# Seven block products in a feed-forward layer: when a chunk's weights are split, where one of their sums lies, and which engine adds one sum

## The chip, the cores and the metric

The kernel runs on one core of a Trainium2 chip. Its engines work side by side, each through its own instructions in order: TensorE (PE, with its weight loads as PEld), VectorE (DVE), ScalarE (ACT), GpSimd (POOL) and SyncE (SP), which issues most DMAs. The metric is the time of one execution in microseconds (us) of the device; lower is better.

## The reference, cut to what matters

The program computes two blocks one after the other; the change lies in the last layer of the second, in its feed-forward part:

```python
def swiglu(h, w_gate, w_up, w_down):
    return (jax.nn.silu(h @ w_gate) * (h @ w_up)) @ w_down

h_lat = h_lat + m_lat[5] * swiglu(modulate(rms_norm(h_lat), m_lat[3], m_lat[4]),
                                  w_ffn_gate[i], w_ffn_up[i], w_ffn_down[i])
```

There are 512 tokens, the width is 1024 and the inner width 2816. Everything is float32.

## The kernel before, in words

**Split products.** A float32 product is made of three matmuls. Each operand is split into a high part (an ACT cast, L239) and a low part (a DVE subtraction, L240), and PE adds high by high, low by high and high by low. `K.split` makes the two parts, `K.wcut` makes them in two tiles (`wh`, `wl`) of a ring for weights, `K.wraw` loads raw weights into a tile (`wr`) of the same kind of ring, and `K.w4` takes such a tile for other data. All three rings are short: an instruction that needs a tile waits until the last reader of the one it replaces is done, and a load is issued only then.

**Chunks.** The inner width is cut into 11 chunks of 256. `gate_up(c)` makes the 256 inner rows of a chunk, in two halves of 128 (`m` = 2c, called A here, and 2c + 1, called B), and leaves them split in `hidh`, `hidl`. `down(c)` multiplies them by the chunk's down weights: eight PSUM results `ob` (four groups of 128 tokens by two halves of the output), each of six matmuls of 512 columns, and each added to `acc` by DVE (L1632). `run` calls `gate_up(c + 1)` before `down(c)`. `ob` has two PSUM buffers, so the third `ob` needs the first to be added to `acc`.

**Seven products.** In this layer (`seven=True`) the weights of an `m` (gate `g`, up `u`, each 1024 by 128) and the tokens (two halves of 256) form a product of 2 by 2 blocks, and it is done with seven block products in place of eight, each of 12 matmuls of 256 columns. `sums` makes the sums of token blocks once (`t1` to `t4`). `prep(m)` makes the sums of weight blocks on POOL: `sb` (L1510), two halves of `sa` (L1511, L1512) and a new low half of `u` (L1513), and splits them. `seven_up(m)` issues the products (PSUM tiles `wa11`, `wa12`, `ws2`, `ws3`, `ws1`, `ws4`, `wa22`) and adds them into c11, c12 (tile `sg`) and c21, c22 (tile `su`): copies on ACT (L1538, L1542 into `m5`), additions from PSUM on DVE (L1539, L1540, L1541, L1546, L1547), and two additions of `m5` on POOL (L1544, L1545). Then come silu on ACT (L1548), the product with c21, c22 on DVE (L1549) and the split into `hidh`, `hidl`.

**What sets the order.** A scheduler arranges each engine's instructions from the order in which the code writes them and from readiness; the result is fixed before the run. `prep(m + 1)` is written in the middle of `seven_up(m)`. The first chunk is done by plain products (`cb`); the chunk before the last ends with POOL's work on `acc` and the residual (L1634, L1635), and the last chunk's down weights are multiplied by the gate on POOL (L955).

Of the kernel before, what the change touches and what calls it, by code (L numbers as in the profile page):

```python
# [7 lines left out]
F32 = mybir.dt.float32  # L8
F32R = mybir.dt.float32r
# [3 lines left out]
ALU = mybir.AluOpType  # L13
# [4 lines left out]
P = 128  # L18
# [8 lines left out]
DFF = 2816  # L27
# [131 lines left out]
class K:  # L159
    def __init__(self, tc, I, out, ctx):  # L160
        self.tc, self.nc, self.I, self.out = tc, tc.nc, I, out
        self.const = ctx.enter_context(tc.tile_pool(name="const", bufs=1))
        self.wp = ctx.enter_context(tc.tile_pool(name="wp", bufs=1))
        self.dram = ctx.enter_context(tc.tile_pool(name="dramp", bufs=1, space=DRAM))
        self.NR, self.NH = 6, 4
        self.nwork = 0
        self.mixed = True
        self.share = False
        self.nl = 0
        self.nrms = 0  # L170
        self.ident = self.load_const("ident")

        self.res = self.const.tile([P, NT, D], F32, name="res")
        self.mhalf = self.const.tile([P, 16], F32, name="mhalf")
        self.nc.gpsimd.memset(self.mhalf, -0.5)
# [134 lines left out]
    def block1(self, mix):  # L310
# [28 lines left out]
        def add(n):  # L339
            for _ in range(n):  # L340
                next(sums, None)
# [1091 lines left out]
GD = (0,)  # L1433


class FFN:


# [11 lines left out]
    def norm(self, si, hs, hn, pool, npool, tag, bufs, ps=None):  # L1450
        nt, row = self.seqs[si]
        w = nt * P
        h, l = ([pool.tile([P, 4 * w], F32R, name=f"{n}{si}{j}", tag=f"fa{si}", bufs=4) for j in range(2)] for n in ("fh", "fl"))
        vh, vl = (lambda k, a=a: a[k // 4][:, (k % 4) * w:(k % 4) * w + w] for a in (h, l))
        self.xs[si] = vh, vl, w
        keep = None
        if self.seven:

            self.F = [[pool.tile([P, 4, 256], F32, name=f"xf{i}{j}", tag="xf", bufs=5) for j in range(2)] for i in range(2)]
            keep = lambda k, pair: self.F[k // 4][pair][:, k % 4, :]  # L1460
        yield from self.K.norm_T(hs, hn, nt, self.layer, 1, row, vh, vl, npool, ps or self.ps, tag, bufs, keep)

    def open(self, pool):
        self.pool = self.hpool = pool
        n = self.off[-1]
        self.acc = [pool.tile([P, D], F32, name=f"acc{tt}", tag="acc", bufs=n) for tt in range(n)]
# [18 lines left out]
    def sums(self):  # L1485

        V, G = self.nc.vector, self.nc.gpsimd
        (f11, f12), (f21, f22) = self.F
        G.tensor_tensor(f11, f12, f11, ALU.subtract)
        V.tensor_tensor(f12, f22, f12, ALU.subtract)  # L1490
        G.tensor_tensor(f22, f22, f11, ALU.subtract)
        V.tensor_tensor(f21, f21, f22, ALU.subtract)
        vh, vl, w = self.xs[0]
        blk = lambda i, j: lambda k: tuple(v(4 * i + k)[:, j * 256:j * 256 + 256] for v in (vh, vl))
        self.B = dict(b11=blk(0, 0), b21=blk(1, 0), b22=blk(1, 1))
        for n, t in (("t3", f12), ("t2", f22), ("t4", f21), ("t1", f11)):
            h = self.hpool.tile([P, 4, 256], F32R, name="xh" + n, tag="xh", bufs=4)
            l = self.pool.tile([P, 4, 256], F32R, name="xl" + n, tag="xf", bufs=5)
            self.K.split(t, h, l)
            self.B[n] = lambda k, h=h, l=l: (h[:, k, :], l[:, k, :])  # L1500

    def prep(self, m):

        if m in self.preps or m >= DFF // P:
            return
        K, G = self.K, self.nc.gpsimd
        g, u = (K.wraw(self.I[n][self.layer, m], (8, P)) for n in ("w_fg", "w_fu"))
        sa, sb = K.w4("sa").rearrange("p (k c) -> p k c", c=P), K.w4("sb")[:, :512].rearrange("p (k c) -> p k c", c=P)
        lo, hi = slice(0, 4), slice(4, 8)
        G.tensor_tensor(sb, u[:, lo], u[:, hi], ALU.add)  # L1510
        G.tensor_tensor(sa[:, lo], sb, g[:, lo], ALU.subtract)  # L1511
        G.tensor_tensor(sa[:, hi], g[:, lo], u[:, lo], ALU.subtract)  # L1512
        G.tensor_tensor(u[:, lo], g[:, hi], sa[:, lo], ALU.subtract)  # L1513
        gs = K.wcut(g, (8, P))
        sh, sl = (self.hpool.tile([P, 8, P], F32R, name=n, tag=n, bufs=2) for n in ("sah", "sal"))
        K.split(sa, sh, sl)
        ss = K.wcut(sb, (4, P))
        us = K.wcut(u, (8, P))
        part = lambda t, o: lambda k: (t[0][:, o + k, :], t[1][:, o + k, :])
        self.preps[m] = dict(a11=part(gs, 0), a12=part(gs, 4), s3=part((sh, sl), 4), s2=part((sh, sl), 0),  # L1520
                             s4=part(us, 0), a22=part(us, 4), s1=part(ss, 0))

    def seven_up(self, m, hid, mi):

        K, ps, pool = self.K, self.ps, self.pool
        V, S, G = self.nc.vector, self.nc.scalar, self.nc.gpsimd
        self.prep(m)
        A, B, w = self.preps.pop(m), self.B, 256

        def product(a, t):  # L1530
            b = ps.tile([P, 512], F32, name="w" + a, tag="gu", bufs=6)[:, :w]
            for k in range(4):
                K.mm3(b, A[a](k), B[t](k), k == 0, k == 3)
            return b
        t, v = (pool.tile([P, 512], F32, name=n, tag="ntf", bufs=3) for n in ("sg", "su"))
        m5 = self.hpool.tile([P, w], F32, name="m5", tag="kp", bufs=1)
        (c11, c12), (c21, c22) = ((a[:, :w], a[:, w:]) for a in (t, v))
        S.copy(c12, product("a11", "b11"))  # L1538
        V.tensor_tensor(c11, c12, product("a12", "b21"), ALU.add)  # L1539
        V.tensor_tensor(c12, c12, product("s2", "t2"), ALU.add)  # L1540
        V.tensor_tensor(c21, c12, product("s3", "t3"), ALU.add)  # L1541
        S.copy(m5, product("s1", "t1"))  # L1542
        self.prep(m + 1)
        G.tensor_tensor(c12, c12, m5, ALU.add)  # L1544
        G.tensor_tensor(c22, c21, m5, ALU.add)  # L1545
        V.tensor_tensor(c12, c12, product("s4", "b22"), ALU.add)  # L1546
        V.tensor_tensor(c21, c21, product("a22", "t4"), ALU.add)  # L1547
        S.activation(t, t, AF.Silu)  # L1548
        V.tensor_tensor(t, t, v, ALU.mult)  # L1549
        K.split(t, hid[0][:, mi, :], hid[1][:, mi, :])  # L1550

    def gate_up(self, c):
        K, I, nc, ps, pool = self.K, self.I, self.nc, self.ps, self.pool
        hid = tuple(self.hpool.tile([P, 2, self.off[-1] * P], F32R, name=n, tag=n, bufs=2) for n in ("hidh", "hidl"))
        if self.seven and c:
            for mi in range(2):
                self.seven_up(2 * c + mi, hid, mi)
            return hid
        jobs = []
        for mi in range(2):  # L1560
            pre = self.pre[mi] if c == 0 and self.pre else None
            W = pre[0] if pre else self.weights(2 * c + mi)
            for si in reversed(range(len(self.xs))):
                if si and pre:
                    o, w = self.off[si] * P, self.xs[si][2]
                    K.split(pre[1], hid[0][:, mi, o:o + w], hid[1][:, mi, o:o + w])
                else:
                    jobs.append((mi, si, W))
        if c == 0 and not self.pre:
            jobs = [(*j, h) for h in (slice(0, 256), slice(256, 512)) for j in jobs]  # L1570
        for mi, si, W, *cut in jobs:
            vh, vl, w = self.xs[si]
            t0 = cut[0].start if cut else 0
            w = 256 if cut else w
            sl = slice(t0, t0 + w)
            o = self.off[si] * P + t0
            if w == 512:
                out = [ps.tile([P, 512], F32, name="gb", tag="gu", bufs=6) for _ in range(2)]
            else:
                cb = ps.tile([P, 2, 256], F32, name="cb", tag="gu", bufs=6)  # L1580
                out = [cb[:, 0], cb[:, 1]]
            for Wt, b in zip(W, out):
                for k in range(8):
                    K.mm3(b, (Wt[0][:, k, :], Wt[1][:, k, :]), (vh(k)[:, sl], vl(k)[:, sl]), k == 0, k == 7)
            t = pool.tile([P, 512], F32, name="sg", tag="ntf", bufs=3)[:, :w]
            nc.scalar.activation(t, out[0], AF.Silu)
            nc.vector.tensor_tensor(t, t, out[1], ALU.mult)
            K.split(t, hid[0][:, mi, o:o + w], hid[1][:, mi, o:o + w])
        return hid
# [662 lines left out]
```

## Time and profile before

| | us |
|---|---|
| median of 3 runs (lowest, highest) | 2409.57 (2403.1, 2412.35) |
| the profiled execution | 2407.82 |
| its span (first to last instruction) | 2406.0 |
| the part of the span with this layer's chunks, and the normalisation ahead of them | 1957 to 2406 |
| eight equal chunks in it | 2050.45 to 2350.35 |

The span is that of one profiled execution; what lies between it and the execution's time is not in the trace. Rows with a time at their start give start and duration of an instruction, and in brackets how long its engine had been idle and which work of which engine ended that. A granted clock of 1.00 is TensorE's level of 2.4 GHz, 0.50 is 1.2 GHz.

### The profile page before, as it was taken

To read this page: it belongs to the slowest core of one execution; us is meant where nothing else is said; L and a number is where in the kernel's file an instruction comes from. 1 tells how busy PE (TensorE), PEld (TensorE's weight loads), DVE (VectorE), ACT (ScalarE), POOL (GpSimd) and SP (SyncE) were. 2 spreads that over 40 slices of the span, in tenths; PEclk is the share of its full clock that TensorE was granted. 3 is DMA by queue.
4 is the path that set the end of the run, shared out by engine and by line. 5 is a ranking of instruction groups with operands and counts; after the bars stand their busy time and mean duration, and the time that the engine had idled before them with its cause. 6 is when DMAs were issued, how large, how long until landed. Compare 5 with 4: busy or idle time off the path is not lost. (4 is left out here: it accounts for less than half of the span.)

```text
span 2406.0 us, 32156 instructions
## 1 busy us (share of the span) xinstructions
PE 2263.3 (94%) x12468; PEld 1730.6 (72%) x12468; DVE 1535.2 (64%) x2511; ACT 840.7 (35%) x1466; POOL 603.4 (25%) x453
## 2 busy tenths in 40 slices
PE   9999899998889978899999999989999988998987
PEld 7667755433567846788888888868767578888886
DVE  7867642524655787675777544665677757667666
ACT  4344422231433242522112111254456534333332
POOL 0011310242330175300000002520211154434346
PEclk9999999999899987999999999999999999988988
DMA  8655698998832012342444311222000232223221
GB/s 290 233 186 181 236 355 333 393 387 308 309 138 70 20 53 97 105 158 88 149 156 151 114 62 53 79 74 88 1 1 1 78 141 71 88 71 101 78 94 44
DMA packets 99160, 339.02 MB, mean 141 GB/s; under 512 B 14373, under 2 KB 16293, under 8 KB 99002
## 3 DMA queue, kind: packets, MB, share of 16 engines
q1 hardware_dynamic: 94394, 324.33, 37.9%
q0 software_dynamic: 4608, 12.59, 1.5%
q8 instruction: 99, 1.62, 0.3%
q14 instruction: 59, 0.48, 0.1%
HBM read 323.21 MB, written 17.86 MB: 142 GB/s over the span
## 5 line engine op out<-in xcount | busy, mean ns | idle before, releaser
L239 ACT CAST wh<-wr 128x1024 fp32r<-128x1024 f32 (+1 forms) x239 | 248.1, 1046 | 515.7 <-PE ob L243 227.7
L240 DVE TENSOR_TENSOR wl<-wr,wh 128x1024 fp32r<-128x1024 f32 (+1 forms) x235 | 316.4, 1353 | 152.2 <-ACT wh L239 149.5
L243 PE MATMUL ob<-wh,hidh 128*128 128x512 f32 x440 | 177.6, 407 | 24.6 <-ACT wh L239 21.6
L243 PE MATMUL ob<-wl,hidh 128*128 128x512 f32 x440 | 176.8, 405 | 8.0 <-DVE wl L240 7.9
L243 PE MATMUL ob<-wh,hidl 128*128 128x512 f32 x440 | 175.2, 401 | 0.0
L1632 DVE TENSOR_TENSOR acc<-acc,ob 128x512 f32<-128x512 f32 x160 | 108.3, 685 | 95.8 <-PE ob L243 95.8
L877 DVE SCALAR_TENSOR_TENSOR adacc<-wr,cond,adacc 128x512 f32<-128x512 f32 x224 | 152.7, 745 | 1.7 <-DMA wr<-in_w_ada 1.7
L1634 POOL TENSOR_TENSOR acc<-acc,gate 128x1024 f32<-128x1024 f32 x10 | 28.1, 2814 | 472.5 <-DVE acc L1632 472.5
L243 PE MATMUL gb<-fh,wh 128*128 128x512 f32 x352 | 139.3, 396 | 0.0
L243 PE MATMUL gb<-fh,wl 128*128 128x512 f32 x352 | 139.2, 396 | 0.0
L243 PE MATMUL gb<-fl,wh 128*128 128x512 f32 x352 | 139.2, 395 | 0.0
L290 POOL TENSOR_TENSOR rs_r<-rs_v,mhalf 128x1 f32<-128x1 f32 (+1 forms) x54 | 47.4, 882 | 328.0 <-DVE rs_v L288 327.8
L243 PE MATMUL gu<-mw,xgT 128*64 128x512 f32 x512 | 125.3, 603 | 0.9 <-issue 0.7
L243 PE MATMUL cb<-fl,wh 128*128 128x256 f32 x416 | 118.7, 285 | 0.0
L243 PE MATMUL cb<-fh,wh 128*128 128x256 f32 x416 | 118.7, 285 | 0.0
L243 PE MATMUL cb<-fh,wl 128*128 128x256 f32 x416 | 117.9, 283 | 0.0
L243 PEld LDWEIGHTS ob<-wh,hidh 128*128 128x128 f32 x440 | 84.7, 195 | 45.0 <-ACT wh L239 23.5
L243 PEld LDWEIGHTS ob<-wl,hidh 128*128 128x128 f32 x440 | 85.0, 193 | 28.1 <-DVE wl L240 10.4
L243 PEld LDWEIGHTS ob<-wh,hidl 128*128 128x128 f32 x440 | 85.2, 194 | 18.6
L243 PEld LDWEIGHTS gu<-mw,xgT 128*64 128x64 f32 x512 | 37.3, 138 | 72.9 <-issue 67.9
L243 PE MATMUL ga<-wl,ah 128*128 128x512 f32 x208 | 84.1, 407 | 3.4 <-DVE wl L240 3.0
L243 PE MATMUL ga<-wh,ah 128*128 128x512 f32 x208 | 85.2, 411 | 1.2 <-ACT cva L1085 1.2
(732 smaller groups left out, 5993.0 us busy)
## 6 DMA issues: line engine op xcount, KB each, us to landing
mw<-in_w_gu SPq DMA_DIRECT2D x128, 512.0 KB
wr<-in_w_ada SPq DMA_DIRECT2D x96, 512.0 KB
mw<-in_w_dn SPq DMA_DIRECT2D x64, 512.0 KB
wr<-in_w_fg SPq DMA_DIRECT2D x44, 512.0 KB
wr<-in_w_fu SPq DMA_DIRECT2D x44, 512.0 KB
wr<-in_w_fd SPq DMA_DIRECT2D x44, 512.0 KB
wr<-in_w_ret SPq DMA_DIRECT2D x28, 512.0 KB
wr<-in_w_in SPq DMA_DIRECT2D x19, 512.0 KB
```

What stands on the lines that cost most here:

```text
L239: self.nc.scalar.copy(h, src)
L240: (eng or self.nc.vector).tensor_tensor(l, src, h.bitcast(F32), ALU.subtract)
L243: self.nc.tensor.matmul(out, lhsT, rhs, start=start, stop=stop, **kw)
L290: nc.gpsimd.tensor_tensor(r, v, self.mhalf[:, :n], ALU.pow)
L877: V.scalar_tensor_tensor(acc[:, r], W[:, k], s, acc[:, r], op0=ALU.mult, op1=ALU.add)
L1632: V.tensor_tensor(a[:, sl], a[:, sl], ob, ALU.add)
L1634: G.tensor_tensor(a, a, gate(tt), ALU.mult)
```

## The change

- `prep(2c)` and `prep(2c + 1)` are both written at the head of `gate_up(c)`, ahead of both `seven_up`, and the chunk's down weights (in `down`) come behind them. `prep` is no longer written in the middle of `seven_up`.
- c12 + `m5` is added by DVE, straight from PSUM (L1560 after), and not by POOL from the copy (L1544 before). POOL keeps c22 = c21 + `m5` (L1561 after).
- The tokens' high and low parts lie in eight tiles of half the size, and the two that hold the block b12, which only the first chunk reads, take the split of `sb` (`s1`) afterwards, two tiles in turn. It leaves the ring of `wh`, `wl`.
- `sb` itself lies in a tile of `xf` (five of them, four in use by the low parts of `t1` to `t4`) and not in the ring of `wr`.

```diff
 class FFN.norm:
-        h, l = ([pool.tile([P, 4 * w], F32R, name=f"{n}{si}{j}", tag=f"fa{si}", bufs=4) for j in range(2)] for n in ("fh", "fl"))
+        if self.seven:
+            self.xpool = pool
+            hb, lb = ([[self.block(n) for _ in range(2)] for _ in range(2)] for n in ("fh", "fl"))
...
+    def block(self, name):
+        return self.xpool.tile([P, 4, 256], F32R, name=name, tag="fa", bufs=8)
 class FFN.prep:
-        if m in self.preps or m >= DFF // P:
-            return
-        sa, sb = K.w4("sa").rearrange(...), K.w4("sb")[:, :512].rearrange(...)
+        sa, sb = (t.rearrange(...) for t in (K.w4("sa"), self.pool.tile([P, 4, 256], F32, name="sb", tag="xf", bufs=5)[...]))
...
-        ss = K.wcut(sb, (4, P))
+        t = self.block("s1").rearrange("p (i a) b -> p i (a b)", i=2)
+        ss = [t[:, i, :].rearrange("p (k c) -> p k c", c=P) for i in range(2)]
+        K.split(sb, *ss)
 class FFN.seven_up:
-        self.prep(m)
...
-        S.copy(m5, product("s1", "t1"))
-        self.prep(m + 1)
-        G.tensor_tensor(c12, c12, m5, ALU.add)
+        b5 = product("s1", "t1")
+        S.copy(m5, b5)
+        V.tensor_tensor(c12, c12, b5, ALU.add)
         G.tensor_tensor(c22, c21, m5, ALU.add)
 class FFN.gate_up:
         if self.seven and c:
+            for mi in range(2):
+                self.prep(2 * c + mi)
             for mi in range(2):
                 self.seven_up(2 * c + mi, hid, mi)
```

POOL in one of the equal chunks, before: a period from the sums of one `m` to the next. Names are tiles, "waits" gives the engines and DMA queues that an instruction waits for; `m_...` is `m5`.

```order
L1544 TENSOR_TENSOR sg<-sg,m_17721 128x256 [waits DVE_49,Activation_49]
L1545 TENSOR_TENSOR su<-su,m_17721 128x256
L1510 TENSOR_TENSOR sb<-wr 128x512 [waits DMAHW7_49,DVE_49]
L1544 TENSOR_TENSOR sg<-sg,m_17854 128x256 [waits DVE_49,Activation_49]
L1545 TENSOR_TENSOR su<-su,m_17854 128x256 [waits Pool_49]
L1511 TENSOR_TENSOR sa<-sb,wr 128x512 [waits DMAHW6_49,DVE_49,Pool_49]
L1512 TENSOR_TENSOR sa<-wr 128x512
L1513 TENSOR_TENSOR wr<-wr,sa 128x512 [waits Pool_49]
```

The same place on POOL, after:

```order
L1527 TENSOR_TENSOR sa<-wr 128x512
L1528 TENSOR_TENSOR wr<-wr,sa 128x512 [waits Pool_49]
L1561 TENSOR_TENSOR su<-su,m_17743 128x256 [waits DVE_49,Activation_49]
L1527 TENSOR_TENSOR sa<-wr 128x512 [waits DMAHW6_49,DMAHW7_49,DVE_49,Pool_49]
L1525 TENSOR_TENSOR sb<-wr 128x512 [waits DVE_49]
L1526 TENSOR_TENSOR sa<-sb,wr 128x512 [waits Pool_49]
L1528 TENSOR_TENSOR wr<-wr,sa 128x512 [waits DMAHW2_49,Pool_49]
L1561 TENSOR_TENSOR su<-su,m_17850 128x256 [waits DVE_49,Activation_49]
L1525 TENSOR_TENSOR sb<-wr 128x512 [waits DMAHW3_49,DVE_49]
```

Each half's sum now stands behind the `prep` instructions of the next chunk that are ready by then; the one instruction that waits for a fresh load of `u` (the last row) stands behind both sums, where before it (third row) stood ahead of B's two.

DVE in the same chunk, before: from the last additions of half B to the additions of the down results (`acc`).

```order
L1546 TENSOR_TENSOR sg<-sg,ws_17953 128x256 [waits PE_49,Pool_49]
L1547 TENSOR_TENSOR su<-su,wa_17967 128x256 [waits DVE_49,PE_49,Pool_49]
L1549 TENSOR_TENSOR sg<-sg,su 128x512 [waits DVE_49,Activation_49]
L240 TENSOR_TENSOR wl<-wr,wh 128x1024 [waits DMAHW4_49,Activation_49]
L240 TENSOR_TENSOR sal<-sa,sah 128x1024 [waits Activation_49]
L240 TENSOR_TENSOR hidl<-sg,hidh 128x512 [waits Activation_49]
L1632 TENSOR_TENSOR acc_15977<-acc_15977,ob 128x512 [waits PE_49]
L1539 TENSOR_TENSOR sg<-sg,wa_18080 128x256 [waits PE_49,Activation_49]
L240 TENSOR_TENSOR wl<-wr,wh 128x1024 [waits DMAHW5_49,Activation_49]
L1632 TENSOR_TENSOR acc_15977<-acc_15977,ob 128x512 [waits PE_49]
```

The same place on DVE, after:

```order
L1560 TENSOR_TENSOR sg<-sg,ws_17907 128x256 [waits DVE_49,Activation_49]
L240 TENSOR_TENSOR s_18076<-sb,s_18076 128x512 [waits PE_49,Activation_49]
L1562 TENSOR_TENSOR sg<-sg,ws_17923 128x256 [waits DVE_49,PE_49]
L1563 TENSOR_TENSOR su<-su,wa_17937 128x256 [waits PE_49,Pool_49]
L1565 TENSOR_TENSOR sg<-sg,su 128x512 [waits DVE_49,Activation_49]
L240 TENSOR_TENSOR wl<-wr,wh 128x1024 [waits DMAHW5_49,Activation_49]
L240 TENSOR_TENSOR hidl<-sg,hidh 128x512 [waits Activation_49]
L1650 TENSOR_TENSOR acc_15977<-acc_15977,ob 128x512 [waits PE_49] x2
```

The sum L1560 has joined DVE's row, neither the weights' low part for the down products nor a sum of the next half stands among the `acc` additions any more, and the first `acc` addition stands behind all of half B's work.

## Rows read from the trace of the kernel before

**Rows 1.** The page: busy time, share and instructions of PE.

```profile
PE 2263.3 (94%) x12468; PEld 1730.6 (72%) x12468; DVE 1535.2 (64%) x2511; ACT 840.7 (35%) x1466; POOL 603.4 (25%) x453
```

**Rows 2.** Stretches: length, busy PE, PEld, DVE, ACT, POOL, granted clock, DMA.

```profile
2050.45:2087.55 37.10, 34.51 (x218) 31.55 (x216) 25.66 (x33) 12.70 (x18) 15.79 (x12) 0.91 0.25 86
...
2312.40:2350.35 37.95, 34.47 (x218) 31.50 (x216) 25.62 (x33) 12.70 (x18) 21.31 (x14) 0.91 0.29 98
```

**Rows 3.** Waits, 1955 to 2406: total us, times, longest us.

```profile
ACT sg L1548 <- DVE sg L1546: 62.0, 20, 14.1
...
DVE sg L1546 <- POOL sg L1544: 34.5, 20, 10.1
...
PE ob L243 <- ACT wh L239: 21.6, 9, 4.4
```

**Rows 4.** POOL in time, in the second of the eight chunks.

```profile
2102.29 1.39 POOL L1510 TENSOR_TENSOR sb<-wr 128x512 f32<-128x512 f32 x1 [6.76 <-DMA wr<-in_w_fu]
2103.64 0.73 POOL L1544 TENSOR_TENSOR sg<-sg,m 128x256 f32<-128x256 f32 x1
2104.33 0.72 POOL L1545 TENSOR_TENSOR su<-su,m 128x256 f32<-128x256 f32 x1
```

**Rows 5.** DVE in time, the same place.

```profile
2101.30 1.23 DVE L240 TENSOR_TENSOR wl<-wr,wh 128x1024 fp32r<-128x1024 f32 x1
2104.41 0.42 DVE L1546 TENSOR_TENSOR sg<-sg,ws 128x256 f32<-128x256 f32 x1 [1.88 <-POOL sg L1544]
...
2106.75 2.31 DVE L240 TENSOR_TENSOR wl<-wr,wh 128x1024 fp32r<-128x1024 f32 x1
```

**Rows 6.** ACT in time: the cast of the down weights, the same place.

```profile
2105.40 1.03 ACT L239 CAST wh<-wr 128x1024 fp32r<-128x1024 f32 x1
```

**Rows 7.** PE in time, the same place, and one gap at the layer's start.

```profile
2103.33 0.28 PE L243 MATMUL wa<-fl,wh 128*128 128x256 f32 x1
...
2104.17 0.28 PE L243 MATMUL wa<-fh,wl 128*128 128x256 f32 x1
2106.48 0.50 PE L243 MATMUL ob<-wh,hidh 128*128 128x512 f32 x1 [2.03 <-ACT wh L239]
...
2109.11 0.80 PE L243 MATMUL ob<-wl,hidh 128*128 128x512 f32 x1 [0.93 <-DVE wl L240]
...
2006.10 0.39 PE L243 MATMUL wa<-fh,wl 128*128 128x256 f32 x1 [1.65 <-DVE wl L240]
```

**Rows 8.** Stretches behind these gaps, columns as in rows 2.

```profile
2107.48:2114.31 6.83, 5.90 (x23) 5.12 (x23) 6.33 (x6) 2.88 (x4) 2.64 (x2) 0.50 0.44 154
...
2005.00:2012.00 7.00, 5.91 (x49) 5.91 (x50) 7.00 (x6) 2.31 (x6) 5.75 (x3) 1.00 0.46 152
```

**Rows 9.** Lines by shape, 2050.45 to 2350.35: total busy, mean ns; idle before.

```profile
L240 DVE TENSOR_TENSOR wl<-wr,wh 128x1024 fp32r<-128x1024 f32 x49 | 70.2, 1432 | 6.7 <-ACT wh L239 6.5
...
L1632 DVE TENSOR_TENSOR acc<-acc,ob 128x512 f32<-128x512 f32 x63 | 42.4, 684 | 43.4 <-PE ob L243 43.4
...
L240 DVE TENSOR_TENSOR sal<-sa,sah 128x1024 fp32r<-128x1024 f32 x16 | 28.3, 1768 | 18.3 <-ACT sah L239 18.1
...
L240 DVE TENSOR_TENSOR wl<-sb,wh 128x512 fp32r<-128x512 f32 x16 | 14.5, 909 | 0.0
```

**Rows 10.** The layer's start: POOL, then two gaps of PE.

```profile
1971.39 2.21 POOL L1510 TENSOR_TENSOR sb<-wr 128x512 f32<-128x512 f32 x1 [1.49 <-DVE wl L240]
...
1979.35 1.53 POOL L290 TENSOR_TENSOR rs_r<-rs_v,mhalf 128x1 f32<-128x1 f32 x1
...
1982.54 1.51 PE L938 MATMUL ntb<-c_ident,acc 128*128 128x128 f32 x6 [5.57 <-DVE acc L918]
...
2032.64 0.79 PE L243 MATMUL ob<-wh,hidh 128*128 128x512 f32 x1 [4.36 <-ACT wh L239]
```

**Rows 11.** The layer's end: DVE's wait for a sum, the first of the last results.

```profile
2367.92 0.42 DVE L1546 TENSOR_TENSOR sg<-sg,ws 128x256 f32<-128x256 f32 x1 [10.13 <-POOL sg L1544]
...
2381.09 1.88 DVE L1625 TENSOR_TENSOR gob<-ob,gate 128x512 f32<-128x512 f32 x3
```

More of the change, by code (lines that the diff above doesn't have):

```diff
@@ L1433, with __init__, __getitem__ @@
 GD = (0,)
+class Halves:
+    def __init__(self, block):
+        self.block = block
+    def __getitem__(self, key):
+        return self.block(key[1].start // 256)
 class FFN:
@@ L1452, in norm @@
         w = nt * P
-        h, l = ([pool.tile([P, 4 * w], F32R, name=f"{n}{si}{j}", tag=f"fa{si}", bufs=4) for j in range(2)] for n in ("fh", "fl"))
-        vh, vl = (lambda k, a=a: a[k // 4][:, (k % 4) * w:(k % 4) * w + w] for a in (h, l))
+        if self.seven:
+            self.xpool = pool
+            hb, lb = ([[self.block(n) for _ in range(2)] for _ in range(2)] for n in ("fh", "fl"))
+            vh, vl = (lambda k, a=a: Halves(lambda j: a[k // 4][j][:, k % 4, :]) for a in (hb, lb))
+            self.b = lambda i, j: lambda k: (hb[i][j][:, k, :], lb[i][j][:, k, :])
+        else:
+            h, l = ([pool.tile([P, 4 * w], F32R, name=f"{n}{si}{j}", tag=f"fa{si}", bufs=4) for j in range(2)] for n in ("fh", "fl"))
+            vh, vl = (lambda k, a=a: a[k // 4][:, (k % 4) * w:(k % 4) * w + w] for a in (h, l))
         self.xs[si] = vh, vl, w
@@ L1492, in sums @@
         V.tensor_tensor(f21, f21, f22, ALU.subtract)
-        vh, vl, w = self.xs[0]
-        blk = lambda i, j: lambda k: tuple(v(4 * i + k)[:, j * 256:j * 256 + 256] for v in (vh, vl))
-        self.B = dict(b11=blk(0, 0), b21=blk(1, 0), b22=blk(1, 1))
+        self.B = dict(b11=self.b(0, 0), b21=self.b(1, 0), b22=self.b(1, 1))
         for n, t in (("t3", f12), ("t2", f22), ("t4", f21), ("t1", f11)):
@@ L1502, in prep @@
     def prep(self, m):
-        if m in self.preps or m >= DFF // P:
-            return
         K, G = self.K, self.nc.gpsimd
         g, u = (K.wraw(self.I[n][self.layer, m], (8, P)) for n in ("w_fg", "w_fu"))
-        sa, sb = K.w4("sa").rearrange("p (k c) -> p k c", c=P), K.w4("sb")[:, :512].rearrange("p (k c) -> p k c", c=P)
+        sa, sb = (t.rearrange("p (k c) -> p k c", c=P) for t in (K.w4("sa"), self.pool.tile([P, 4, 256], F32, name="sb", tag="xf", bufs=5)[:, 0:2, :].rearrange("p a b -> p (a b)")))
         lo, hi = slice(0, 4), slice(4, 8)
```

## The prediction

> **What bounds the kernel now.** I read the page first: PE is busy 94% of the span [rows 1]. That average hides the layer that the change touches, so next the stretches. The eight equal chunks last 37.5 us each, (2350.45 - 2050.45) / 8 with a rounding of 0.1 at the last edge, and in each PE is busy about 34.5 us at a granted clock of 0.91, not 1.00 [rows 2]. So each chunk has a stall and a piece at half clock. The waits say whose stall it is: ScalarE's silu waits for DVE's sum L1546 in all 20 halves (62.0 us), DVE's sum waits for POOL's sum L1544 (34.5), and PE's first down product waits for the cast of the down weights (21.6) [rows 3]. One chunk in time shows how these hang together. POOL waits 6.76 us idle for a load of `u`, L1510 runs at 2102.29, and only then comes L1544, though its own operands were there [rows 4]. DVE adds at 2104.41 after an idle time behind POOL [rows 5]; silu follows on ACT, behind it the cast of the down weights at 2105.40 [rows 6]; PE stands still for 2.03 us until 2106.48 and for 0.93 us until 2109.11 [rows 7]. Then 6.83 us run at 0.50 [rows 8]. Price of a chunk's stall: 2.03 + 0.93 + 6.83 / 2 = 6.4 us. What is left, 37.5 - 6.4 = 31.1, is PE at full clock: 168 matmuls at 0.12 (seven starts in 0.84 us, [rows 7]) are 20.2, which leaves 10.9 for 48 matmuls of 512 columns, 0.23 each, 1.37 per down product.
>
> **The change part by part.** *The wait that goes.* In the order of POOL after, both sums L1561 stand ahead of the `sb` that waits for a fresh load of `u`; c12 + `m5` isn't there at all. The chain load, L1510, L1544, L1546, silu, cast is cut twice. The down weights' cast and subtraction also come behind both halves' weights in ScalarE's and DVE's order but ahead of the products by a whole half, so 2.03 and 0.93 both go, and with them the half clock: up to 6.4 us a chunk.
>
> *The sum on DVE.* Two additions per chunk at 0.42, the price of every addition from PSUM here [rows 5], 0.84 us; POOL loses two of 0.73 [rows 4]. In the shared time of DVE and POOL the 128x1024 subtraction takes 1.23 alone and 2.31 beside POOL [rows 5], so what shares matters more than what is added. The Trainium skill, page "SBUF — State Buffer", section "Who interferes with whom", says that a VectorE instruction with at most one SBUF input does not contend with GpSimd, and one with two does. The row agrees: L1546 took 0.42 while POOL's L1545 ran from 2104.33 on [rows 4, 5]. If L1560 did contend, each would cost a turn of 1.08 more, and the first addition below would come 2.2 later in a chunk.
>
> *Buffers.* `sb` and `s1` leave the two rings, so loads can be issued earlier; no instruction is added for it. I put no gain of its own on it, since [rows 4] shows the load as the late one only for the instruction that now has no sum behind it. If it is late still, it delays `sa`, not the sum; cover for this is a whole half, 10 us.
>
> *The wait that comes.* Before, DVE's first `acc` addition stood two rows behind a subtraction, among the next half's sums. After, the first `acc` addition stands behind everything of half B, and the eight down products stand together on PE. `ob` has two buffers: the third product waits for the first addition. I count from the end of the last down product. PE is done with A and B after 159 x 0.12 = 19.0 (nine of A's 168 ran earlier), with two down products at 21.8, with nine matmuls of the next half at 22.8. That is when the third product is due. DVE first finishes the previous chunk's last subtraction and last addition, at 1.7, and then has until the first `acc` addition 5 `wl` and 2 `sal` of 128x1024, two `s1` and two L1565 of 512, two `hidl`, 12 additions from PSUM, and that addition itself. At before's mean prices [rows 9]: 5 x 1.43 + 2 x 1.77 + 4 x 0.91 + 2 x 0.68 + 12 x 0.42 + 0.68 = 21.4, so 23.1. Its inputs are not all there in time (`sal` waits for POOL and the ACT cast, the last sums for PE). Going through the order row by row with turns taken between DVE and POOL I come to 24.6. Lower bound: from the last product at 19.0 DVE needs 0.3 + 0.42 + 0.68 + 1.23 + 0.68 + 0.68 = 4.0, so 23.0, a stall of next to nothing. Upper bound: prices alone, 7 x 1.23 + 6 x 0.68 + 12 x 0.42 + 0.68 = 18.4, and each of POOL's ten instructions of a chunk costing DVE a turn of 1.08: 1.7 + 18.4 + 10.8 = 30.9, a stall of 8.1. I take 24.6, a stall of 1.8, since it is nearest to the mean prices of before.
>
> *The clock behind the new stall.* A single gap of 1.65 us in this layer is followed by 1.00; the pair 2.03 and 0.93 by 0.50 [rows 7, 8]. 1.8 lies between them. I take one chunk in eight with the loss of 3.4, 0.4 on average.
>
> *Sum of a chunk:* 31.1 + 1.8 + 0.4 = 33.3, against 37.5: 4.2 less, in eight chunks 33.6.
>
> *The layer's start.* Four `prep` instructions from 1971.39 hold up the tiny rs_r until 1979.35, and PE is idle 5.57 for it [rows 10]. After, only one of them, L1527, stands ahead of rs_r; some 5.5 us come forward. The `prep` of the first two halves then comes behind `sums`, and DVE's second addition of half A stands behind the `sal` of half B, three POOL instructions and a cast later; I take 4 us back for that. The gap of 4.36 before the first down product [rows 10] is the stall of the other chunks in a bigger form, and 4.36 + 3.4 gives way to about 2 to 3.5. Together 5.5 - 4 + 4.5 = 6, between 0 and 12.
>
> *The layer's end.* POOL multiplies and adds `acc` into the residual in four pairs, and both kernels have the last sums behind that. Before, L1546 waits 10.13 for it, and from there to the first last result DVE needs 13.2 (2367.92 to 2381.09, [rows 11]). After, c12 doesn't wait, only c21 does (L1563, behind L1561), and from L1563 the list to the first result is 3 `wl`, two L1565 and two `hidl`, 7 additions: 3 x 1.23 + 4 x 0.68 + 7 x 0.42 = 9.4. That is 3.8 less, and a little less at half clock: 5, between 0 and 9.
>
> *Total:* 33.6 + 6 + 5 = 44.6 against the profiled execution of 2407.8 (span 2406.0 and 1.8 around it): 2363. The median of the runs shown is 1.75 above that execution: **2365**.
>
> **The rivals.** *(a) PE alone sets the chunk.* If DVE keeps to the lower bound, no stall comes in place of the old one: 31.1, 6.4 less per chunk, 51 + 11 = 62, so 2347. For it: DVE is busy only 25.7 of 37.5 now [rows 2]. Against: the mean prices already give 23.1, past the due time.
>
> *(b) The new stall costs the clock.* The same stall, but 3.4 behind it in every chunk: 31.1 + 1.8 + 3.4 = 36.3, 1.2 less per chunk, 9.5 + 11 = 20.5: 2389. For it: 1.8 is nearer to 2.03 than I'd like, and the row by row count can be off by 1. Against: the gap of 1.65. The Trainium skill's page "TensorE: Matmul & The Clock Gate", section "A second HAM failure mode: psum-queue depth-cycling", speaks for this rival: it tells of a kernel whose PE goes idle briefly but often between groups while it cycles through PSUM banks, and whose clock swings for it. The trace of before has no chunk whose only wait is for a bank, so it neither agrees nor disagrees.
>
> *(c) The sum is freed, but its queue is late all the same.* POOL still makes c22, and L1563 waits for it. If L1527, which waits for two loads, is as late as L1510 was, L1561 of half B is, and through L1563 and L1565 the hidden rows. Then a chunk stays at 37.5, only start and end gain: 2409.6 - 11 = 2398.5, within 0.5%. For it: POOL's wait for a load was 6.76 in a chunk. Against: in the order the fresh load stands behind both sums.
>
> *(d) DVE loses its turns: slower.* One mechanism: POOL's ten instructions now all run inside A and B, where DVE's work before the first `acc` addition is one row. If all seven 128x1024 subtractions take 2.31 and the inputs cost 2 more, the first addition is done at 1.7 + 18.4 + 7 x 1.08 + 2 = 29.7, the third product is 6.9 late, and the clock falls: 31.1 + 6.9 + 3.4 = 41.4, 3.9 more per chunk, 31 - 11 = 20 more: 2430. It decides from an addition at 27.2 on (31.1 + 4.4 + 3.4 = 37.5 + 11 / 8).
>
> **How the numbers follow.** Forecast 0.50 (2350 to 2378), (b) 0.22 (to 2398), (a) 0.10 (from 2342), (c) 0.11, (d) 0.07. The range leaves out (c) and (d), 0.18: 2342 to 2398. Half a percent, 12 us, is about what a measurement of this kernel can tell from none; faster by more is the forecast, (a) and (b), 0.82; within, (c), 0.11; slower, (d), 0.07.
>
> **What would show it.** Right: chunks of 33 to 34 us; no wait of L1562 or silu for POOL; no PE wait for the cast of down weights, but one of 1 to 2.5 us for a DVE `acc` addition at the third down product; the clock at 0.50 in few chunks; rs_r some 5 us earlier. Wrong: chunks of 31 without a wait for `acc` (a); 0.50 behind each (b); L1563 waiting for L1561 for microseconds (c); most `wl` above 2 us and the first addition over 4 us late (d). The prediction fails most easily where I counted DVE and POOL turn by turn, since a shift of 1 us there decides between forecast and (b).

## The result and the profile after

The changed kernel takes 2377.22 us (median of 4 runs, 2366.97 to 2385.43), the kernel before 2407.91 (4 runs, 2403.1 to 2412.35). The ratio is 0.987 with a 95% interval of 0.982 to 0.992: faster by 1.3%, 12 us above the forecast of 2365, inside the range of 2342 to 2398. The span of the profiled execution fell from 2406.0 to 2370.6.

The equal chunks first. The columns are those of rows 2: length, busy PE, PEld, DVE, ACT, POOL, granted clock, DMA. The edges are the ends of a chunk's last down product; the first line holds all eight, the second what follows, and the last two are the pieces just behind a stall. The line ahead of them shows the eight chunks of the kernel before; its edges are the ends of the last down product too, 0.16 behind those of [rows 2], with the same length.

```profile
2050.61:2350.51 299.90, 274.70 (x1731) 251.10 (x1730) 205.22 (x257) 101.57 (x144) 131.77 (x99) 0.91 0.26 87
```

```profile
2045.91:2317.73 271.82, 255.99 (x1734) 235.90 (x1733) 221.34 (x273) 101.99 (x144) 145.63 (x83) 0.98 0.28 94
2317.73:2370.60 52.87, 41.78 (x255) 36.67 (x254) 33.92 (x47) 13.13 (x21) 30.89 (x21) 0.96 0.10 40
...
2079.28:2112.55 33.27, 31.38 (x218) 29.01 (x218) 27.48 (x35) 12.73 (x18) 17.04 (x10) 1.00 0.29 96
2112.55:2147.47 34.92, 32.94 (x219) 30.17 (x218) 27.66 (x35) 12.78 (x18) 17.04 (x10) 0.95 0.27 91
...
2137.49:2140.91 3.42, 3.42 (x9) 2.65 (x9) 1.01 (x2) 0.00 (x0) 1.28 (x1) 0.50 0.33 125
2172.32:2180.90 8.58, 8.58 (x37) 6.95 (x38) 4.18 (x7) 1.05 (x1) 1.28 (x1) 1.00 0.15 56
```

Against [rows 2] the mean chunk is 34.0 us (271.82 / 8) instead of 37.5: about 4 us shorter in the five where the clock stays at 1.00, and about 2.5 shorter in the three where it falls. The waits from 1955 on, to be read against [rows 3]:

```profile
ACT sg L1564 <- DVE sg L1562: 55.6, 19, 4.2
...
PE ob L243 <- DVE acc L1650: 15.8, 8, 2.6
...
PE ob L243 <- DVE acc L1648: 9.3, 1, 9.3
...
DVE su L1563 <- POOL su L1561: 8.4, 1, 8.4
```

PE's wait for the cast of the down weights (21.6 in 9 waits before) is no longer among the long ones, nor DVE's for POOL's sum in each half; c21 waits for POOL once, at the end. In their place PE waits once in each of the eight chunks, 15.8 / 8 = 2.0 us on average, for an `acc` addition of DVE, and once for 9.3 in the chunk ahead of them. In time, PE:

```profile
1976.31 0.85 PE L938 MATMUL ntb<-c_ident,acc 128*128 128x128 f32 x6 [1.17 <-DVE acc L918]
...
2034.94 0.79 PE L243 MATMUL ob<-wh,hidh 128*128 128x512 f32 x1 [9.30 <-DVE acc L1648]
...
2103.89 0.49 PE L243 MATMUL ob<-wh,hidh 128*128 128x512 f32 x1 [1.89 <-DVE acc L1650]
...
2137.27 0.63 PE L243 MATMUL ob<-wh,hidh 128*128 128x512 f32 x1 [1.98 <-DVE acc L1650]
...
2172.32 0.50 PE L243 MATMUL ob<-wh,hidh 128*128 128x512 f32 x1 [2.10 <-DVE acc L1650]
```

POOL, the same chunk as in [rows 4], and rs_r as in [rows 10]:

```profile
1975.09 0.55 POOL L290 TENSOR_TENSOR rs_r<-rs_v,mhalf 128x1 f32<-128x1 f32 x1 [2.36 <-DVE rs_v L288]
...
2097.31 1.59 POOL L1561 TENSOR_TENSOR su<-su,m 128x256 f32<-128x256 f32 x1 [2.09 <-DVE su L1557]
2106.02 1.29 POOL L1525 TENSOR_TENSOR sb<-wr 128x512 f32<-128x512 f32 x1 [7.12 <-DMA wr<-in_w_fu]
```

POOL still waits 7.12 us for the load of `u`, as it did before (6.76), but the sum has passed ahead of that wait by 8.7 us. And DVE: in the first chunk, in the chunk that ends at 2112.55, and at the end.

```profile
2032.64 1.32 DVE L240 TENSOR_TENSOR sal<-sa,sah 128x1024 fp32r<-128x1024 f32 x1 [3.12 <-ACT sah L239]
2033.88 0.41 DVE L1563 TENSOR_TENSOR su<-su,wa 128x256 f32<-128x256 f32 x1
2034.21 0.68 DVE L1648 COPY acc<-ob 128x512 f32<-128x512 f32 x1
...
2092.29 1.78 DVE L240 TENSOR_TENSOR hidl<-sg,hidh 128x512 fp32r<-128x512 f32 x1
...
2102.56 0.69 DVE L240 TENSOR_TENSOR hidl<-sg,hidh 128x512 fp32r<-128x512 f32 x1
2103.16 1.28 DVE L1650 TENSOR_TENSOR acc<-acc,ob 128x512 f32<-128x512 f32 x2
...
2335.91 0.42 DVE L1563 TENSOR_TENSOR su<-su,wa 128x256 f32<-128x256 f32 x1 [8.37 <-POOL su L1561]
...
2345.63 1.88 DVE L1643 TENSOR_TENSOR gob<-ob,gate 128x512 f32<-128x512 f32 x3
```

The first `acc` addition of the chunk begins at 2103.16, right behind the low part of half B's hidden rows, and the third down product starts as it ends. The same subtraction of 512 columns takes 0.69 at 2102.56, with POOL idle, and 1.78 at 2092.29, with POOL busy.

### The profile page after: what moved, and what is told of

Its sections match the earlier page's. It is cut to its first block, busy times and chain, and to the rows that moved or that the text cites. A ratio compares the mean times of both kernels' runs of the same rounds, so it can differ in the third digit from the quotient of the medians.

```text
span 2370.6 us, 32226 instructions
## 1 busy us (share of the span) xinstructions
PE 2239.8 (94%) x12468; PEld 1708.4 (72%) x12468; DVE 1551.7 (65%) x2531; ACT 841.4 (35%) x1466; POOL 612.4 (26%) x433
## 4 chain that ended last, share of the span: by engine, by line
PE 66%; DVE 10%; POOL 4%; issue 4%; ACT 2%; DMA 1%; SPq 0%; POOLq 0%; DVEq 0%; ACTq 0%
PE gb L243 13%; PE ob L243 12%; PE ga L243 10%; PE cb L243 5%; PE gu L243 5%; PE ws L243 3%; PE sc L243 3%; PE yb L243 3%; PE wa L243 2%; PE ptb L1924 2%; DVE wl L240 2%; POOL rs_r L290 1%; PE kb L243 1%; ACT wh L239 1%; PE vb L243 1%
## 5 line engine op out<-in xcount | busy, mean ns | idle before, releaser
L240 DVE TENSOR_TENSOR wl<-wr,wh 128x1024 fp32r<-128x1024 f32 (+1 forms) x235 | 332.0, 1419 | 152.0 <-ACT wh L239 149.5
L243 PE MATMUL ob<-wh,hidh 128*128 128x512 f32 x440 | 177.3, 403 | 28.1 <-DVE acc L1650 15.8
L1652 POOL TENSOR_TENSOR acc<-acc,gate 128x1024 f32<-128x1024 f32 x10 | 28.1, 2810 | 465.1 <-DVE acc L1650 465.1
L243 PEld LDWEIGHTS ob<-wl,hidh 128*128 128x128 f32 x440 | 84.2, 191 | 17.4
```

The lines of the kernel that those rows point to most:

```text
L240: (eng or self.nc.vector).tensor_tensor(l, src, h.bitcast(F32), ALU.subtract)
L243: self.nc.tensor.matmul(out, lhsT, rhs, start=start, stop=stop, **kw)
L1652: G.tensor_tensor(a, a, gate(tt), ALU.mult)
```

## Experiments

Theory, from the two traces: the old stall was a queue on POOL (sums behind a wait for a load), and what sets a chunk now is DVE's list up to the first `acc` addition against two PSUM buffers. Rivals: it is the sum's move to DVE alone, the code's order alone, or the tiles alone; and for the new stall, that DVE and POOL taking turns bound the chunk as a whole. "Chunk" is the mean of the same eight chunks, from the end of the first to the end of the ninth down step; ratios are to the runs of the kernel before on the same chip.

| kernel | median us | ratio (95%) | chunk us |
|---|---|---|---|
| before | 2407.91 | 1 | 37.5 |
| changed | 2377.22 | 0.987 (0.982, 0.992) | 34.0 |
| tiles and order (sum back on POOL) | 2379.93 | 0.989 (0.986, 0.993) | 34.1 |
| sum alone | 2384.24 | 0.991 (0.989, 0.994) | 34.7 |
| sum and tiles | 2390.82 | 0.993 (0.990, 0.995) | 35.5 |
| tiles alone | 2394.73 | 0.995 (0.993, 0.997) | 36.0 |
| sum and order | 2408.8 | 1.002 (1.000, 1.004) | 37.5 |
| order alone | 2416.72 | 1.005 (1.003, 1.007) | 38.9 |

### The parts, one by one and in pairs

**The sum back on POOL.**

```diff
-        V.tensor_tensor(c12, c12, b5, ALU.add)
+        G.tensor_tensor(c12, c12, m5, ALU.add)
```

> The changed kernel with one part undone: c12 + m5 is added by POOL from the copy again. Queue theory (PE's old stall hung on the sum standing behind a load's wait in POOL's order; in the new order no sum stands there, wherever it is added): the gain stays, 2370 to 2390, PE's only wait in a chunk is the third down product for an acc addition, 1.5 to 3 us. Sum theory (the gain is the sum's move to DVE): 2400 to 2410, silu waits for POOL again.

The gain stays. All eight chunks:

```profile
2048.82:2321.77 272.95, 252.86 (x1733) 233.56 (x1733) 227.28 (x257) 102.76 (x144) 162.67 (x99) 0.99 0.27 93
```

272.95 / 8 = 34.1 against 34.0. With tiles and order in place no sum stands behind a load, and the gain doesn't hang on who adds it. The sum theory falls as the whole reason. The two chunks are alike for unlike reasons, though. PE's waits for the `acc` addition, from 2090 to 2250:

```profile
PE ob L243 <- DVE acc L1650: 12.9, 5, 2.7
```

Over all eight chunks they are 2.5 us on average where the changed kernel has 2.0, but the clock falls behind one of them and not behind three. So the sum on DVE is worth about 0.5 us of wait in a chunk, and in these two executions the clock hides it.

**The sum alone.**

```diff
 (before)
-        S.copy(m5, product("s1", "t1"))
+        b5 = product("s1", "t1")
+        S.copy(m5, b5)
         self.prep(m + 1)
-        G.tensor_tensor(c12, c12, m5, ALU.add)
+        V.tensor_tensor(c12, c12, b5, ALU.add)
```

> The kernel before with only the sum c12 + m5 moved to DVE, read from PSUM. Sum theory: most of the gain, 2372 to 2385. Queue theory: silu and the cast of the down weights come free of POOL, so the gap of 2.03 us goes, but c22 and with it c21's addition still stand behind the load on POOL, and DVE's low part of the down weights behind them; a chunk of 35 to 37 us, 2385 to 2405.

2384, on the border of the two and better than the queue theory had it. Eight chunks, PE in one of them, and DVE's wait for POOL in it:

```profile
2046.63:2324.53 277.90, 257.69 (x1730) 232.52 (x1730) 206.03 (x273) 101.11 (x144) 127.65 (x82) 1.00 0.28 93
```

```profile
2101.18 0.50 PE L243 MATMUL ob<-wl,hidh 128*128 128x512 f32 x1 [1.15 <-DVE wl L240]
2105.14 0.50 PE L243 MATMUL ob<-wh,hidh 128*128 128x512 f32 x1 [0.75 <-ACT wh L239]
2106.30 0.50 PE L243 MATMUL ob<-wh,hidh 128*128 128x512 f32 x1 [0.67 <-DVE acc L1633]
```

```profile
2098.82 0.42 DVE L1548 TENSOR_TENSOR su<-su,wa 128x256 f32<-128x256 f32 x1 [1.03 <-POOL su L1546]
```

The mechanism is as expected: silu and the cast come free, c21 still waits 1.03 for POOL behind the load. What was underrated is the clock. The gap of 2.03 and the one of 0.93 have become three of 1.15, 0.75 and 0.67, and the granted clock is 1.00 over all eight chunks. Per chunk PE's idle time falls from 3.15 us (299.90 - 274.70, over eight) to 2.53, and its busy time, which holds the half clock, from 34.3 to 32.2. So most of the 2.75 us that a chunk gains comes from the clock and not from the gaps.

**The order alone.**

```diff
 (before)
-        self.prep(m + 1)
 ...
+            for mi in range(2):
+                self.prep(2 * c + mi)
             for mi in range(2):
                 self.seven_up(2 * c + mi, hid, mi)
```

> The kernel before with only both preps written at the head of a chunk (same rings, sum on POOL). In its order on POOL the sb of the next chunk, with its load's wait, still stands ahead of half B's two sums. Theory that the code's order is what pays: 2372 to 2385. Queue theory: the wait is kept, 2395 to 2410.

Slower than before, which neither had. Eight chunks, and POOL and PE in the second:

```profile
2045.97:2356.82 310.85, 267.22 (x1730) 243.32 (x1730) 218.52 (x257) 102.44 (x144) 138.51 (x100) 0.92 0.24 82
```

```profile
2092.91 1.30 POOL L1510 TENSOR_TENSOR sb<-wr 128x512 f32<-128x512 f32 x1 [18.45 <-DMA wr<-in_w_fu]
```

```profile
2113.55 0.79 PE L243 MATMUL ob<-wh,hidh 128*128 128x512 f32 x1 [5.47 <-DVE acc L1633]
```

On the old rings the load of `u` comes later still: POOL waits 18.45 us for it with the sums behind it, DVE's list is late for them, and the third down product waits 5.47.

**The tiles alone.** The new places of `sb` and `s1`, with `prep(m)` and `prep(m + 1)` back in `seven_up` and the sum on POOL.

> The kernel before with only the new places of s1 and sb (prep in its old places in the code, sum on POOL). Its order on POOL has the sums ahead of the sb that waits for a load, and PE does both halves before the down products, as in the changed kernel. Queue theory: most of the gain without the sum's move and without the new code order, 2372 to 2390. Sum theory and code-order theory: no gain, 2400 to 2410.

A gain, but a smaller one than expected. Eight chunks, and a wait from 2090 to 2250:

```profile
2050.95:2339.07 288.12, 264.05 (x1717) 239.11 (x1717) 228.86 (x257) 103.03 (x143) 151.51 (x96) 0.95 0.27 90
```

```profile
PE ob L243 <- ACT wh L239: 7.5, 4, 2.0
```

The sums pass ahead of the load, but the down weights' cast is still written behind the weights of the next half, and PE waits for it (1.9 a chunk). That is the part that only the new order takes away.

**Sum and order, without the tiles.** The order alone, and the sum as above.

> The changed kernel without the new places of s1 and sb: prep at the head of a chunk and the sum on DVE, on the rings of before. The order alone took 38.9 us a chunk (its third product waited 5.4 for an acc addition; sums behind the load's wait on POOL), the sum alone 34.7. If the tiles are what the new order needs, since c22 and c21 still stand behind the sb that waits for a load: chunks of 36 to 39, 2390 to 2415. If the sum's move is enough in any order: 34 to 35, 2375 to 2388.

```profile
2044.77:2344.76 299.99, 263.11 (x1731) 240.61 (x1730) 223.68 (x273) 102.57 (x144) 127.57 (x84) 0.95 0.25 85
```

The waits in these chunks:

```profile
POOL sb L1510 <- DMA wr<-in_w_fu: 156.0, 11, 18.1
...
PE ob L243 <- DVE acc L1634: 36.9, 8, 5.0
...
DVE su L1547 <- POOL su L1545: 9.3, 9, 1.2
```

37.5, nothing gained: freeing c12 is not enough in this order. POOL still waits up to 18.1 us for the load of `u` with c22 and the other work behind it, and the third down product waits 4.6 on average. c21's own wait for c22 is only about 1 us, so it is a part of this; what makes the rest was not taken apart. The tiles are what the order needs.

**Sum and tiles, without the order.** The tiles alone, and the sum as above.

> The changed kernel with prep in its old places in the code (in the middle of seven_up), so sum and tiles without the new order. The tiles alone took 36.0 a chunk, with the first down product waiting for the cast of its weights (about 1.9 and 1.2) since the weights of the next half are written ahead of it. Queue theory: that wait hangs on the weights' place and not on the sum, so it stays in part: 34.5 to 36, 2380 to 2395. Sum theory: 34 as in the changed kernel, 2372 to 2382.

```profile
2053.14:2336.81 283.67, 261.54 (x1727) 236.88 (x1727) 229.49 (x273) 103.33 (x143) 135.25 (x81) 0.97 0.27 92
```

```profile
2110.23 0.50 PE L243 MATMUL ob<-wh,hidh 128*128 128x512 f32 x1 [1.41 <-ACT wh L239]
2112.55 0.77 PE L243 MATMUL ob<-wl,hidh 128*128 128x512 f32 x1 [0.88 <-DVE wl L240]
```

35.5: the wait for the down weights stays, wherever the sum is. So the parts don't add up. Two ways lead out of the queue, the sum on DVE or tiles and order together, and the change walks both; the second alone already brings a chunk to 34.1, against 34.0 with both.

### The new stall

**Banks for the third and fourth product.** The edit moves every second group of tokens, so the seventh and eighth product go to the other banks as well.

```diff
 (changed kernel, run's add)
-                    ob = prod(tt, n_, *tag[0])
+                    ob = prod(tt, n_, *(('gu', 6) if self.seven and c < nch - 2 and tt % 2 else tag[0]))
```

> The changed kernel, but the down products of every second group of tokens lie in PSUM banks of the gate and up products (six of them) and not in the two of the others, so the third and the fourth need no addition to be done. List theory (the new stall is DVE's list up to the first acc addition against two buffers): no stall in the chunks, 31.1 to 32 us each instead of 34.0, no half clock, 2350 to 2362 in all. Rival (DVE and POOL taking turns are the bound as a whole, the buffer is only where it shows): the wait goes to another place, chunks stay at 33.5 to 34.5, 2370 to 2385.

2357.63 (2357.0 to 2358.18), ratio 0.981 (0.979, 0.983).

```profile
2048.71:2298.76 250.05, 249.54 (x1730) 231.34 (x1730) 220.44 (x273) 103.34 (x144) 132.59 (x82) 1.00 0.31 102
2298.76:2355.20 56.44, 44.14 (x265) 39.23 (x263) 34.49 (x47) 13.23 (x21) 33.73 (x22) 0.94 0.10 38
```

250.05 / 8 = 31.3, PE busy in all but 0.5 us of 250, at 1.00. The list theory holds, and the floor of 31.1 that the prediction worked out is confirmed to 0.2. The end is 3.6 us longer than in the changed kernel (56.44 against 52.87). The turns of DVE and POOL are not the bound: with the stall gone DVE is busy 220 of 250 us and keeps up.

**More on DVE.** Two more additions from PSUM in each half.

```diff
+        V.tensor_tensor(c22, c11, b5, ALU.add)
+        V.tensor_tensor(c22, c12, b5, ALU.add)
         V.tensor_tensor(c12, c12, b5, ALU.add)
```

> The changed kernel with two more additions of 0.42 us from PSUM on DVE in each half (into c22, which POOL overwrites): 1.7 us a chunk, of which the order gives 0.7 back ahead of the first acc addition (the low part of half B stands behind it now). List theory: the stall grows by 1.0 to 2.9, chunks of 35 and up to 38.4 with half clock behind each, 2380 to 2410. Rival (something else sets the third product's time, such as the down weights or POOL): chunks stay at 34, 2370 to 2382.

```profile
2043.05:2330.69 287.64, 263.94 (x1730) 241.73 (x1730) 221.76 (x305) 104.00 (x144) 126.24 (x84) 0.95 0.27 88
```

36.0 a chunk, 2385.33 in all, with stalls of 2.6 to 3.7 for the `acc` addition, 3.0 on average: the third product's time moves with DVE's list, by the 1.0 that was expected. The other 1.0 of the chunk goes with the clock, 0.95 instead of 0.98.

**Both sums on DVE.**

```diff
-        S.copy(m5, b5)
         V.tensor_tensor(c12, c12, b5, ALU.add)
-        G.tensor_tensor(c22, c21, m5, ALU.add)
+        V.tensor_tensor(c22, c21, b5, ALU.add)
```

> The changed kernel with c22 + m5 on DVE from PSUM too; ScalarE's copy m5 is gone and POOL adds neither. List theory: DVE's list is 0.84 us longer per chunk, the stall 2.7 instead of 1.9, at the end c21 no longer waits behind POOL's residual work (the gap of 2.6 goes): 2372 to 2390. Turns theory: two instructions fewer on POOL, so DVE gains up to 2 us a chunk: stall under 1, 2350 to 2368.

```profile
2048.05:2322.36 274.31, 255.50 (x1730) 235.45 (x1730) 223.51 (x289) 97.55 (x128) 119.38 (x67) 0.98 0.28 93
2322.36:2373.70 51.34, 41.48 (x255) 36.43 (x253) 40.65 (x49) 12.47 (x19) 30.87 (x19) 0.93 0.10 41
```

```profile
2108.27 0.50 PE L243 MATMUL ob<-wh,hidh 128*128 128x512 f32 x1 [2.26 <-DVE acc L1648]
```

2376.97. The stall is 2.3, between the theories (2.7 and under 1): DVE's list is 0.84 longer and the stall only about 0.35; that POOL's two instructions fewer give back the rest fits, but isn't shown apart. The end is 1.5 us shorter.

**The down products in two parts.** Four behind half A and four behind half B.

> The changed kernel with the eight down products in two parts, four behind half A and four behind half B (the left and the right half of the output). List theory: DVE has only half the list before the first acc addition of a part, so the third product of a part waits 0 to 1 us, chunks 31.5 to 33, 2352 to 2370. Rival (turns are the bound): 33.5 to 35.

```profile
2044.47:2332.81 288.34, 260.40 (x1731) 238.51 (x1730) 215.82 (x272) 104.06 (x144) 116.76 (x80) 0.97 0.28 88
```

```profile
2095.31 0.50 PE L243 MATMUL ob<-wh,hidh 128*128 128x512 f32 x1 [2.21 <-DVE acc L1652]
```

36.0, 2383.53: a miss for both. The third product of a part now waits for an addition that stands behind all of a half's list. Four chunks have two waits (2.21 here, 1.30 in the part behind it), the others one of 2.0 to 3.1: twelve waits with 27.9 us in all, where the changed kernel has eight with 15.8. Half the list is short, but so is the time until it is due.

**Banks and both sums together, and the first chunk.** Third and fourth product in the other banks and both sums on DVE:

> The changed kernel with the third and fourth down product in the other banks (31.3 us a chunk, the end 4.3 late for c22 behind POOL's residual work) and both sums on DVE from PSUM. List theory: 0.84 more on DVE's list is covered now, chunks stay at 31.2 to 31.6; at the end c21 waits for nothing on POOL, 3 to 5 us less: 2350 to 2356. If DVE is the bound with no stall left: chunks of 32, 2358 to 2364.

```profile
2040.47:2293.82 253.35, 250.56 (x1731) 231.17 (x1730) 225.50 (x289) 99.15 (x128) 114.04 (x67) 1.00 0.29 100
2293.82:2347.00 53.18, 42.68 (x264) 37.62 (x263) 42.52 (x49) 12.58 (x19) 32.70 (x19) 0.95 0.10 40
```

2352.79, ratio 0.978 (0.975, 0.981), inside what the list theory expected: the end takes 53.2 instead of 56.4. But the chunks take 31.7, just above its 31.6 (one has a wait of 1.96 at its end), and in the profiled executions this eats what the end gives: both kernels need 306.5 for the two stretches. That the second sum on DVE adds anything to the banks is not shown, as the two intervals overlap. Then the copies of the first chunk's results from ScalarE:

```diff
-                        V.tensor_copy(a[:, sl], ob)
+                        (self.nc.scalar.copy if self.seven else V.tensor_copy)(a[:, sl], ob)
```

> As the third of these, and the first chunk's eight down results are copied to acc by ScalarE, not by DVE, whose list there waits for the sums of the chunk after next. If DVE's place in line is what makes the gap of 6.5 to 9.3 us in the first chunk: 3 to 5 us less than that kernel, 2346 to 2353. If the cast of those sums on ScalarE, which waits for the same POOL work, stands ahead of the copies as well: within 2 us of it.

```profile
2035.21 0.79 PE L243 MATMUL ob<-wh,hidh 128*128 128x512 f32 x1 [4.43 <-ACT acc L1646]
```

2352.16, the same within the interval (0.978; 0.975 to 0.981). The gap is 4.43 instead of 6.40, but ScalarE's copies stand behind the cast of the same sums, as the second expectation had it. These two beat the changed kernel by 1%; which of them is better, and whether either beats the banks alone, was not told apart.

## Why the prediction was right

**The stall that went.** Right. The 6.4 us of a chunk were the queue, the cast and the clock; with the new wait taken away as well, a chunk is 31.3, where 37.5 - 6.4 = 31.1 was worked out. The prediction put no gain of its own on the buffers, though. Without the new tiles the other two parts gain nothing (37.5 a chunk), so the order on POOL that it read had their effect in it already.

**The stall that came.** Right to 0.1 in the chunk of rows above: the first addition was to be done, and the third product to start, 24.6 after the last down product. It started 2103.89 - 2079.28 = 24.6 after it. In all eight chunks it is 24.6 to 25.3. The stall was to be 1.8 and is 1.6 to 2.6, 2.0 on average. The steps of that count were not put down, only the sum at mean prices (23.1) and the bounds (23.0 and 30.9), so how it came to 24.6 can't be compared; in the chunk of rows above the five `wl` take 9.2 where mean prices gave 7.2, and the two `sal` 2.7 for 3.5. The Trainium skill, page "SBUF — State Buffer", section "Who interferes with whom", says that a VectorE instruction with two SBUF inputs contends with a GpSimd instruction that reads SBUF. The subtraction of 512 columns at 1.78 beside POOL instead of 0.69 agrees, and [rows 5] had shown the same difference for 1024 columns.

**The clock behind it.** Too small, as the floor and the stall were, each by about 0.2 us, and the length of the gap, by which it was judged, doesn't decide. One chunk in eight was to lose 3.4. In the profiled execution three of eight lose 3.4 / 2 = 1.7 each, 0.64 on average instead of 0.4: 31.3 + 2.0 + 0.6 = 33.9, measured 34.0, forecast 33.3. Three chunks for one at half the price each: that the sum comes close is in part luck. Rival (b) was thus true of three chunks, at half its price, and false of five. The section "A second HAM failure mode: psum-queue depth-cycling" of the Trainium skill's page "TensorE: Matmul & The Clock Gate" speaks of brief waits between groups, by PSUM banks, that swing the clock. The trace agrees in three chunks of eight, and the clock is 1.00 in all eight once the wait for the bank is taken away; but with the sum alone, where each chunk has three waits of 0.7 to 1.15, it is 1.00 as well. Eight chunks gained 28.1 where 33.6 was forecast.

**The layer's start.** 4.7 for 6 (2050.61 to 2045.91), but by other steps, and 0.9 of it stands ahead of the change: PE's first transposition of this layer (L938) already begins at 1956.60 instead of 1957.47. rs_r came 4.3 earlier, PE's gap of 5.57 became 1.17. What was given back lies elsewhere: the gap of 4.36 was to give way to 2 to 3.5 and became 9.30. That this leaves a gain is, among other things, because two of the eight down products now stand ahead of it: from its end to the end of the chunk it is 11.0 us (2034.94 to 2045.91) where it was 18.0 (2032.64 to 2050.61). DVE has the `sal` of the next chunk's half B ahead of this half B's last sum and of the first copy to `acc`, and waits 3.12 for it (2032.64). I had put that cost on half A, and not at the third down product.

**The layer's end.** 2.6 for 5. From c21's addition to the first last result it is 9.7 (2335.91 to 2345.63) where 9.4 was counted; from c12's it was 13.2 before. But c21's addition comes 0.8 later than c12's did, counted from the end of the eighth chunk (2335.91 - 2317.73 = 18.2 against 2367.92 - 2350.51 = 17.4), as one of POOL's multiplications of the last weights by the gate now stands ahead of its residual work, and the 1.2 for the clock didn't come. These two make up 2.0 of the 2.4 that are missing.

**The sum.** In the profiled executions the gain is 28.1 + 4.7 + 2.6 = 35.4 us where 44.6 was forecast. The other 3 of the 12 us are scatter: the profiled execution of the changed kernel lies 4.9 below its median, where 1.75 was taken.

**The other rivals.** (a) came true only with the banks. (c) did not: c21 waits for POOL once, 8.37 at the end. (d) did not: the first addition was at 24.6, not at 27.2. What a late first addition costs is real: with 1.7 us more on DVE a chunk went to 36.0, and the order without the tiles came to the turning point (38.9), there behind POOL's wait of 18.45 us for a load and not by the turns alone that (d) counts.

## What to carry to other kernels

A helper engine's queue is read by what stands behind its waits for loads: a short sum behind such a wait can hold up other engines (here 6.8 us idle on POOL stood behind 3 us of idle PE and 3.4 lost at half clock in a chunk), and it comes free by moving the sum or by moving what waits. When a stall goes, count the list of the engine that must return the next buffer up to the instruction that returns it, row by row with the turns it takes with a neighbour; here that gave the new stall to 0.2 us on average, and other banks for half of the products removed it. Parts of a change that serve the same end need not add up, and one alone can lose (the order without the tiles).

## What the runs showed of the hardware that was not expected

The length of a gap of TensorE does not tell whether the clock falls behind it: in the changed kernel one of 1.98 us is followed by 3.42 us at 0.50, one of 2.10 by 1.00, and with the sum back on POOL seven of eight gaps of 2.2 to 2.7 are followed by full clock. With the sum alone three gaps of 0.7 to 1.15 us in each chunk left it at 1.00. What decides it was not found.

The time of a single run says little about one such spell: the four runs of the changed kernel lie 18 us apart, and the profiled executions of all kernels reach this layer (first L938 transposition) between 1953 and 1963 us, ahead of anything that they do differently there. The four runs with the banks alone lie 1.2 us apart, but those of the two last kernels, with hardly a wait either, 7 and 5, so the spread can't be put down to this clock.
